# The attention section of a two-layer decoder trunk in another written-out order of its 1,026 steps

## The chip, the cores and the metric

The kernel runs on one core of one Trainium2 chip. The metric is the device time of one execution in microseconds. Shown are the median and the spread of three runs, and one profiled execution from which every row below is taken.

## What is computed

The reference is a decoder trunk with two layers for 256 tokens of width 1024, all in float32: a recurrent block, an MLP, sparse attention, an MLP, each behind an RMS norm and added to the residual, and a last norm.

```python
D_MODEL, SEQ, DEPTH, D_FF, N_HEADS, HEAD_DIM = 1024, 256, 2, 4096, 16, 64
def reference(...):
    for i in range(DEPTH):
        h = _rmsnorm(x, norm_mix[i])
        x = x + (_rglru_mixer(h, ...) if i % 2 == 0 else _nsa_mixer(h, ...))
        h = _rmsnorm(x, norm_ffn[i])
        x = x + jnp.square(jax.nn.relu(h @ mlp_w_up[i])) @ mlp_w_down[i]
    return _rmsnorm(x, norm_final)
# _nsa_mixer: q, six key/value projections and gates from h @ w_in; three branches
# (compressed keys, selected blocks, sliding window), each a masked softmax with
# ALiBi slopes, times its gate; their sum (16 heads x 64) @ w_out
```

## The kernel before

**Numbers in two parts.** Float32 products are made of parts: a value is its rounded part "hi" and the rest "lo", and x·w is hi·hi + hi·lo + lo·hi. Each weight piece (128x1024, 512 KB) is loaded into one of five buffers `raw0` to `raw4` by the queue of the SyncE engine (SP), rounded to `hi` by ScalarE (ACT) or VectorE (DVE) ("hi-split", L426), and its rest is made by VectorE ("lo-split", `whl<-raw,whl`, L423; L369 in the MLP). Piece i lies in `raw[i mod 5]`, and in one of seven hi/lo pairs in the tile `whl`. Four pieces (`BY_DMA`) are made otherwise: the GpSimd queue (POOL) loads hi with a cast, an engine multiplies it by -1 into lo (L491), and a second POOL transfer adds the weights to it (L493).

**The attention section** (L920 to the end of `trunk_kernel`'s second block) does the projections (`ks0 kw0 q0 ...`), the scores, softmax steps (L1297 is the rescaling of a block of probabilities), transposes with a copy `pth` (L1311), the products with the values (L1340, gathered into `osum` by L1344 on ACT and L1347 on DVE, then split into `oh` and `ol`), and the output projection in two halves `out0` and `out1` of eight column blocks m0 to m7. Each block of `out1` ends in a bank of the product memory and is added to the residual `xt` by DVE (L633, `xt<-xt,bank`). Blocks m0 to m7 of `out1` use the banks 2, 3, 4, 0, 1, 2, 3, 4.

**The lead-in.** The section's last part holds the first four pieces of the second MLP's up-projection, up1.0 to up1.3 (weight pieces 117 to 120, banks 0 to 3, 24 products of 128x256 each, L413 to L415), the norm for it (`hhl`, `acc`, L552 to L568), and, under `ahead`, the splits of the next three pieces 121 to 123 (`raw1`, `raw2`, `raw3`), which only the MLP behind the section reads. Piece 117 is in `raw2`, 118 in `raw3`, 119 in `raw4`, 120 in `raw0`; the last half of `out1`'s weights (`o13`, for m6 and m7) is piece 116, one of the four made by POOL.

**What sets the order.** A section collects its steps with `add(...)`; a step has one or two engines that may run it, and a function that issues its instructions. `emit` then calls the steps one by one. Each engine runs its instructions in the order in which they were issued, and each queue of transfers as well; waits between engines follow from the data. For the attention section the order is the text `ORDER`: step numbers, where `'` takes a step's second engine.

```python
sec.add("dve", 1.14, diff(lo, raw, hi), ...)      # a lo-split, one step
sec.emit(ORDER)                                    # the section's last line
```

Of the kernel before, what the change touches and what calls it, by code (L numbers as in the profile page):

```python
# [37 lines left out]
W1T, THS, THD, TPV, THT, NEARLY = 8.0, 10.5, 6.4, 44.0, 5.6, 6  # L38
SEED = (45, 94848, 51544, 88889, 49550, 67068, 32457, 33019)
ORDER = """  # L40
2 4 10 11 19 7 20 1 21 6 82 22 30 88 12 75 13 31 14 15 181 32 89 16 33 17 23 90 92 34 41 38' 35 24' 27 40 42 98 83 43 44
99 194 50 223 164 45 51 242 28' 36 46' 52 26 25 47 39 53 29 18 37 69 54 71 165 64 57 59 183 70 62 73 321 65 55 76 60 67
72 56 78 68 184 74 61 77 63 123 196 48' 79 376 58 80 126 124 81 66 49 118 84 225 121 85 197 86 127 94 122 87 119 426 108
125 96 109 91 226 114 93 128 153 120 148 110 129 95 154 480 244 133 97 9 130 151 135 0 101 131 3 134 103 323 100 149 102
136 142 137 105 111 152 207 115 141 104 156 106 139 324 140 107 166 157 378 167 138' 143 245 168 155 161 147 379 158 505
112 169 162 566 185 116 170 159 612 113 186 172 163 187 428 160 146' 212 144' 174 145' 188 213 173' 150 220 198 221 208
189 482 217 175 429 199 190 200 117 171 678 201 191' 193 227 202 222 192 228 204' 218 229 205 215 230 176 219 206 180'
# [6 lines left out]
422 342 486 360 473 435' 361 343 444 509 362 345 447 344 415 718 363 346 445 487 364 418 471 455 719 365 488 366 419  # L54
347' 456 367 416 489 457 368 402 348 474 490 417 369 570 494 492 458 405 401' 571 478 406 449 436 459 460 407 450 475
479 495 510 408 461 453 438 572 409 462 476 440 452 537 451 464 463 497 573 538 465 467 442 466 539 534 904 511 468 574
535 784 499 512 575' 454 500 536 502 524 529 513 501 503 761 585 588 514 540 887 515 530 541 519 586 525 542 531 520 527
616 532 545 587 517 528 617 888 543 522 631 533 618 965 589 546 619 576 526 544 632 590 973 504 591 560 633 596 981 547
927 549 594 561 580 592 658 583 548 563 550 595 599 578 682 593 551 597 581 600 634 552 620 564 648 553 562 565' 701 635
554 649 598 555 685 651 636 556 652 691 621' 686 606 557 688 624 607 650 659 626 608 558 687 629 610 660 559 692 689 627  # L60
601 694 663 602 622 690 661 603 611 928 710 738 609 604 711 713 605 695 989 712 906 653 1003 664 637 662 714 656 665 654
724 657 638 666 696 655 639 715 683 786 667 640 702 668 699 672 641 787 669' 725 642 671 684 945 700 643 726 697 721 644
# [3 lines left out]
823 818 796 837 833 821 835 807 794' 824 795' 822 819 789 825 817 842 802 803 808 797' 834 826 804 843 845 827 840 790  # L66
805 844 846 830 831' 847 848 828 841 838 863 806 836 849 829' 839 947' 850 864 866 857 791 896 948 867 858 865 859 909
861' 862 860' 853 868 869 851 917 854 870 852 872 871 889 873 875 874 809 876 855' 967' 877 856 929 880 878 897 881 983
890 879 918 882' 930 975 883 910 968 931 891 898 892 919 1007 899 911 937 900 912 1005 976 938 939 950 893 1006 895 1011
951 884 958 894 952 901 959 960 932 1009 1015 984 915 1010 991 1018 933 940 977 902 953 913 992 985 941 1016 920 1020  # L70
961 903 1022 914 923 1024 916 921 934 962 922 993 954 924 935 969 942 943 963 994 936 955 978 956 944 970 957 964 979
1013' 980 997 1014 971 998 986 999 1000 972 995 1001 996 1002 987 1017 988
"""
ROUNDS, SHIFT, MOVES, SPREAD = 6, 1.5, 12, 3.0
HPEN, LPEN, APEN, LEAD = 0.56, 1.0, 0.0, 9.0
# [1491 lines left out]
```

## Time and profile before

| what | value |
|---|---|
| median of three runs | 563.41 us (563.34 to 563.67) |
| the profiled execution's own time | 563.77 us |
| its span in the trace | 562.0 us (1.77 us lie around it) |
| attention section on TensorE (PE), by the timeline | 254.84 to 395.17 us |
| busy share of the span: PE / DVE / ACT / POOL | 98% / 81% / 69% / 9% |
| mean granted clock of TensorE | 0.993 |

Times in rows are microseconds from the start of the span unless they say ns. A row of a timeline is: start, duration, engine, source line, operation, output<-inputs, shape, count of instructions in the row, and in brackets the idle time of the engine just before it and what ended it. TensorE's products are pipelined: a product's duration is longer than its distance to the next one.

### The profile page before, as it was taken

Reading aid. Unit: us, or ns where it says so; the run is one execution under the profiler, and the core shown is the slowest. Engines: PE = TensorE matmul, PEld = TensorE weight load, DVE = VectorE, ACT = ScalarE, POOL = GpSimd, SP = SyncE. Lnnn points to the kernel's source line nnn. Section 1 sums busy time; section 2 is a strip of 40 time slices with the busy share of each in tenths; the row PEclk is TensorE's granted clock in tenths of the full one; section 3 lists DMA queues with packets and bytes.
Section 4 is the critical chain, followed back from the end, with each engine's and each line's share of the span. In section 5 each row is a group of like instructions: output and inputs, shape, how many; then the busy total and the mean of one; then the engine's idle time right before and its main releaser. Section 6 shows DMA issues by size and latency. Waiting matters only on the chain.

```text
span 562.0 us, 10531 instructions
## 1 busy us (share of the span) xinstructions
PE 549.1 (98%) x3862; PEld 517.2 (92%) x3862; DVE 455.8 (81%) x946; ACT 387.4 (69%) x790; POOL 51.1 (9%) x63
## 2 busy tenths in 40 slices
PE   9999999999999999999999998998999999999994
PEld 8999999999999999999999997998999999999994
DVE  6999999999995665767999999998899996565532
ACT  7699776877775543545999999974887776453420
POOL 1210000000000211311000101000000000142220
PEclk9999999999999999999999999998999999999998
DMA  8936366665555566556642585445576566456402
GB/s 300 398 125 197 147 224 204 247 219 188 206 207 188 180 207 212 186 187 229 237 152 66 154 234 168 96 94 195 166 234 213 197 213 217 160 193 212 157 1 75
DMA packets 32611, 105.19 MB, mean 187 GB/s; under 512 B 3984, under 2 KB 6944, under 8 KB 32560
## 3 DMA queue, kind: packets, MB, share of 16 engines
q1 hardware_dynamic: 30784, 99.70, 52.4%
q0 software_dynamic: 1200, 4.29, 3.4%
q8 instruction: 30, 0.49, 0.3%
q10 hardware_dynamic: 576, 0.53, 0.3%
q14 instruction: 21, 0.17, 0.1%
HBM read 101.36 MB, written 1.05 MB: 182 GB/s over the span
## 4 chain that ended last, share of the span: by engine, by line
PE 93%; DVE 2%; ACT 2%; DMA 1%; issue 1%; SPq 0%; DVEq 0%
PE bank L419 35%; PE bank L420 18%; PE bank L415 9%; PE bank L413 9%; PE bank L414 9%; PE bank L790 2%; PE bank L1308 2%; PE bank L1335 1%; PE bank L1268 1%; PE bank L1269 1%; DMA raw<-in_dram 1%; DVE whl L423 1%; PE bank L1139 1%; PE bank L1140 1%; PE bank L1138 1%; ACT whl L426 1%
## 5 line engine op out<-in xcount | busy, mean ns | idle before, releaser
L369 DVE TENSOR_TENSOR whl<-raw,whl 128x1024 fp32r<-128x1024 f32 x117 | 146.5, 1272 | 5.9 <-ACT whl L360 3.1
L419 PE MATMUL bank<-hhl,whl 128*128 128x512 f32 x456 | 149.4, 382 | 0.0
L419 PE MATMUL bank<-uhl,whl 128*128 128x512 f32 x448 | 146.8, 382 | 0.0
L360 ACT CAST whl<-raw 128x1024 fp32r<-128x1024 f32 (+1 forms) x118 | 120.5, 1046 | 7.8 <-ACT whl L360 5.7
L420 PE MATMUL bank<-hhl,whl 128*128 128x256 f32 x456 | 124.3, 273 | 0.0
L420 PE MATMUL bank<-uhl,whl 128*128 128x256 f32 x448 | 122.1, 273 | 0.0
L419 PEld LDWEIGHTS bank<-hhl,whl 128*128 128x128 f32 x456 | 86.2, 189 | 11.9
L419 PEld LDWEIGHTS bank<-uhl,whl 128*128 128x128 f32 x448 | 84.7, 189 | 11.8
L413 PE MATMUL bank<-hhl,whl 128*128 128x256 f32 x312 | 88.9, 285 | 1.7 <-DVE xt L633 1.7
L420 PEld LDWEIGHTS bank<-hhl,whl 128*128 128x128 f32 x456 | 87.6, 192 | 0.0
L415 PE MATMUL bank<-hhl,whl 128*128 128x256 f32 x312 | 86.9, 279 | 0.4 <-DVE whl L423 0.2
L414 PE MATMUL bank<-hhl,whl 128*128 128x256 f32 x312 | 86.8, 278 | 0.0
L420 PEld LDWEIGHTS bank<-uhl,whl 128*128 128x128 f32 x448 | 86.0, 192 | 0.0
L633 DVE TENSOR_TENSOR xt<-xt,bank 128x256 f32<-128x256 f32 x40 | 16.1, 414 | 72.3 <-ACT part L921 58.8
L423 DVE TENSOR_TENSOR whl<-raw,whl 128x1024 fp32r<-128x1024 f32 (+3 forms) x69 | 72.4, 1071 | 0.7 <-ACT whl L426 0.4
L413 PEld LDWEIGHTS bank<-hhl,whl 128*128 128x128 f32 x312 | 60.4, 194 | 2.2 <-issue 1.9
L426 ACT CAST whl<-raw 128x1024 fp32r<-128x1024 f32 (+2 forms) x62 | 58.0, 957 | 6.4 <-DMA raw<-in_dram 3.8
L415 PEld LDWEIGHTS bank<-hhl,whl 128*128 128x128 f32 x312 | 60.5, 194 | 1.0 <-DVE whl L423 1.0
L414 PEld LDWEIGHTS bank<-hhl,whl 128*128 128x128 f32 x312 | 60.4, 194 | 0.6 <-DVE hhl L683 0.2
L921 ACT COPY part<-bank 128x256 f32<-128x256 f32 x14 | 5.2, 373 | 61.8 <-PE bank L420 61.8
L886 ACT COPY b<-bank 128x256 f32<-128x256 f32 x57 | 21.0, 368 | 21.4 <-PE bank L420 21.3
L893 ACT ACTIVATE u<-t 128x256 f32<-128x256 f32 x64 | 26.7, 418 | 10.6 <-DVE t L891 5.0
(222 smaller groups left out, 998.3 us busy)
## 6 DMA issues: line engine op xcount, KB each, us to landing
raw<-in_dram SPq DMA_DIRECT2D x171, 512.0 KB, 4.1
whl<-in_dram POOLq DMA_DIRECT2D x8, 512.0 KB, 5.6
gw<-in_dram SPq DMA_DIRECT2D x4, 512.0 KB, 8.3
raw<-in_dram SPq DMA_DIRECT2D x5, 256.0 KB, 5.1
xt<-in_dram SPq DMA_DIRECT2D x4, 256.0 KB, 4.3
zwol<-in_dram SPq DMA_DIRECT2D x2, 512.0 KB, 5.8
raw<-in_dram SPq DMA_DIRECT2D x2, 456.0 KB, 4.0
kh<-th SPq DMA_DIRECT2D x8, 64.0 KB, 2.2
```

Of the source, the lines that this page charges most:

```text
L360: (act.copy if eng is None else eng.tensor_copy)(hi_t[i % NSPL][:, :n], raw_t[i % NRAW][:, :n])
L369: (eng or dve).tensor_tensor(lo[:, :n], raw_t[i % NRAW][:, :n], hi[:, :n].bitcast(F32), op=OP.subtract)
L413: pe.matmul(ps, wh, xh, start=start, stop=False)
L414: pe.matmul(ps, wh, xl, start=False, stop=False)
L415: pe.matmul(ps, wl, xh, start=False, stop=stop)
L419: pe.matmul(z.rearrange("p (i b a) -> p i b a", i=2, a=2), wh, xd, start=start, stop=False)
L420: pe.matmul(pairs(z[:, :S]), wl, xd[:, 0], start=False, stop=stop)
L423: return lambda e: e.tensor_tensor(o, a, h.bitcast(F32), op=OP.subtract)
L426: return lambda e: (e.copy if e is act else e.tensor_copy)(o, a)
L633: dve.tensor_tensor(two(xt[:, m]), two(xt[:, m]), nat(z), op=OP.add)
L886: act.copy(two(b), nat(z[:, S:]))
L893: act.activation(u, t, AF.Square)
```

## The change

Only the text `ORDER` differs. It holds 958 numbers, those of the 1,026 steps that issue something on an engine or a queue (the other 68 stand for the transfers that they start); the same 958 stand in another order, 41 of them with the other choice of engine. Products, shapes and buffers are the same; the lines of numbers tell nothing by themselves, so the first two are shown, and then what three places of the resulting programs look like.

```diff
@@ -38,38 +38,38 @@
 ORDER = """
-2 4 10 11 19 7 20 1 21 6 82 22 30 88 12 75 13 31 14 15 181 32 89 16 33 17 23 90 92 34 41 38' 35 24' 27 40 42 98 83 43 44
+1 4 11 19 7 10 20 2 21 3 22 30 88 12 75 13 31 14 82 15 181 89 32 16 33 17 23 90 98 91 24' 83 92 41 27 18 42 34 194 29 43
...
```

**VectorE at the end of the section, before.** These are its instructions from the split of piece 118 on (`raw3`); `raw4` is piece 119 (up1.2), `raw0` piece 120 (up1.3), `raw1` and the `raw2` here are the pieces 121 and 122 that only the MLP reads. `bank1_..` to `bank4_..` are the blocks of `out1`, `hhl` is the norm's lo part.

```order
L423 TENSOR_TENSOR whl_84<-raw3_81,whl_84 128x1024
L423 TENSOR_TENSOR whl_84<-raw1_79,whl_84 128x1024
L553 SCALAR_TENSOR_TENSOR hhl_93<-xt_88,vec_87,hhl_93 128x256 x2
L633 TENSOR_TENSOR xt_88<-xt_88,bank1_4560 128x256
L423 TENSOR_TENSOR whl_84<-raw4_82,whl_84 128x1024
L423 TENSOR_TENSOR whl_84<-raw2_80,whl_84 128x1024
L633 TENSOR_TENSOR xt_88<-xt_88,bank2_4609 128x256
L633 TENSOR_TENSOR xt_88<-xt_88,bank3_4626 128x256
L423 TENSOR_TENSOR whl_84<-raw0_78,whl_84 128x1024
L633 TENSOR_TENSOR xt_88<-xt_88,bank0_4521 128x256
L633 TENSOR_TENSOR xt_88<-xt_88,bank4_4641 128x256
```

**The same place of VectorE with the change**, from the split of piece 119 to that of piece 120.

```order
L423 TENSOR_TENSOR whl_84<-raw4_82,whl_84 128x1024
L553 SCALAR_TENSOR_TENSOR hhl_93<-xt_88,vec_87,hhl_93 128x256 x2
L633 TENSOR_TENSOR xt_88<-xt_88,bank2_4611 128x256
L633 TENSOR_TENSOR xt_88<-xt_88,bank0_4494 128x256
L423 TENSOR_TENSOR whl_84<-raw3_81,whl_84 128x1024
L553 SCALAR_TENSOR_TENSOR hhl_93<-xt_88,vec_87,hhl_93 128x256 x3
L633 TENSOR_TENSOR xt_88<-xt_88,bank3_4638 128x256
L563 TENSOR_TENSOR acc_94<-acc_94,sq1_99 128x256
L553 SCALAR_TENSOR_TENSOR hhl_93<-xt_88,vec_87,hhl_93 128x256
L423 TENSOR_TENSOR whl_84<-raw0_78,whl_84 128x1024
```

Further on, these are VectorE's last five rows of the section with the change; the next one is the MLP's first.

```order
L568 TENSOR_TENSOR acc_94<-acc_94,sq1_99 128x256
L423 TENSOR_TENSOR whl_84<-raw1_79,whl_84 128x1024
L544 RECIPROCAL rcol_96<-rcol_96 128x2
L423 TENSOR_TENSOR whl_84<-raw2_80,whl_84 128x1024
L423 TENSOR_TENSOR whl_84<-raw3_81,whl_84 128x1024
```

The splits of the pieces 121, 122 and 123 now stand behind the norm's last sum, the residuals of the banks 2 and 0 stand before the split of piece 118, and that of piece 119 stands ahead of it.

**ScalarE at the end of the attention, before**: the last two copies of transposes, the copies of the last value product, and the hi-splits of the pieces 119 and 118.

```order
L1311 CAST pth_2885<-bank5_4516 128x384
L1311 CAST pth_2885<-bank6_4531 128x384
L1344 COPY osum_2882<-bank7_4544 64x256 x2
L426 CAST whl_84<-raw4_82 128x1024
L426 CAST whl_84<-raw3_81 128x1024
```

**The same with the change.**

```order
L1311 CAST pth_2885<-bank5_4515 128x384
L1311 CAST pth_2885<-bank6_4520 128x384
L491 ACTIVATE whl_84<-whl_84 128x1024
L426 CAST whl_84<-raw3_81 128x1024
L1344 COPY osum_2882<-bank7_4545 64x256 x2
```

The multiplication by -1 of piece 116 (L491), which stood on VectorE, is now here, between the transposes' copies and the copies of the last value product; so is the hi-split of piece 118.

**The queue of SyncE while the last queries are moved, before**: `sa`, `sb` are the halves of the queries' tiles, filled by moves from `th` and `tl`; the others are loads of weight pieces.

```order
L346 DMA raw2_80<-in_4_dram 128x1024
L465 DMA sa2_2860<-th1_2875 64x256
L346 DMA raw3_81<-in_4_dram 128x1024
L346 DMA raw4_82<-in_4_dram 128x1024
L465 DMA sb2_2864<-tl1_2877 64x256
L465 DMA sb2_2864<-th1_2875 64x256
L465 DMA sa2_2860<-tl1_2877 64x256
L465 DMA sb3_2865<-th0_2874 64x256
```

**The same with the change.**

```order
L346 DMA raw2_80<-in_4_dram 128x1024
L465 DMA sa2_2860<-tl1_2877 64x256
L465 DMA sb2_2864<-tl1_2877 64x256
L465 DMA sa2_2860<-th1_2875 64x256
L465 DMA sa3_2861<-th0_2874 64x256
L465 DMA sb3_2865<-th0_2874 64x256
L465 DMA sb2_2864<-th1_2875 64x256
L465 DMA sb3_2865<-tl0_2876 64x256
L465 DMA sa3_2861<-tl0_2876 64x256
L346 DMA raw3_81<-in_4_dram 128x1024
L346 DMA raw4_82<-in_4_dram 128x1024
```

The loads of the pieces 118 and 119 (`raw3`, `raw4`) moved from between the moves of the last two queries to behind all of them.

## Rows read from the trace of the kernel before

**Rows 1.** The page's first section: busy time, share of the span and number of instructions of each engine.

```profile
PE 549.1 (98%) x3862; PEld 517.2 (92%) x3862; DVE 455.8 (81%) x946; ACT 387.4 (69%) x790; POOL 51.1 (9%) x63
```

**Rows 2.** Busy time in five stretches of the section. The columns are the stretch and its length, then the busy time (and number of instructions) of PE, the weight loads PEld, DVE, ACT and POOL, the granted clock of TensorE, the busy share of the transfer engines, and GB/s.

```profile
267.00:300.00 33.00, 33.00 (x280) 32.66 (x279) 32.38 (x86) 31.64 (x74) 0.87 (x6) 1.00 0.47 165
300.00:330.00 30.00, 29.57 (x244) 28.55 (x243) 28.85 (x119) 27.88 (x86) 2.79 (x5) 1.00 0.57 156
330.00:346.00 16.00, 14.52 (x105) 12.77 (x104) 15.73 (x66) 15.85 (x51) 0.00 (x0) 1.00 0.68 206
346.00:371.20 25.20, 25.20 (x201) 23.94 (x201) 24.42 (x106) 22.80 (x77) 3.21 (x4) 1.00 0.48 102
379.70:390.50 10.80, 8.86 (x61) 8.51 (x62) 10.70 (x23) 6.02 (x14) 0.00 (x0) 0.84 0.59 207
```

**Rows 3.** TensorE's timeline from its first product of the lead-in (up1.0) to a product of the MLP's fourth piece; `hhl,whl` is a product of up1, L419 one of the MLP behind the section.

```profile
379.65 0.35 PE L413 MATMUL bank<-hhl,whl 128*128 128x256 f32 x1
...
380.28 0.28 PE L415 MATMUL bank<-hhl,whl 128*128 128x256 f32 x1
382.25 0.35 PE L413 MATMUL bank<-hhl,whl 128*128 128x256 f32 x1 [1.70 <-DVE xt L633]
...
383.10 0.28 PE L414 MATMUL bank<-hhl,whl 128*128 128x256 f32 x1
383.62 0.58 PE L415 MATMUL bank<-hhl,whl 128*128 128x256 f32 x1 [0.25 <-DVE whl L423]
...
387.14 0.27 PE L413 MATMUL bank<-hhl,whl 128*128 128x256 f32 x1
...
390.38 0.28 PE L415 MATMUL bank<-hhl,whl 128*128 128x256 f32 x1
...
395.17 0.38 PE L419 MATMUL bank<-hhl,whl 128*128 128x512 f32 x1
...
403.03 0.38 PE L419 MATMUL bank<-hhl,whl 128*128 128x512 f32 x1
```

**Rows 4.** TensorE alone in four stretches of that time: stretch, length, its busy time (number of products), granted clock, busy share of the transfer engines, GB/s.

```profile
379.60:382.20 2.60, 0.95 (x7) 1.00 0.33 104
382.20:383.60 1.40, 1.13 (x8) 1.00 0.76 296
383.60:387.10 3.50, 3.48 (x16) 0.51 0.73 229
387.10:390.45 3.35, 3.35 (x32) 1.00 0.58 234
```

**Rows 5.** VectorE's timeline at the end of the section and into the MLP.

```profile
372.13 0.85 DVE L1347 TENSOR_TENSOR osum<-osum,bank 64x256 f32<-64x256 f32 x2 [0.61 <-ACT osum L1344]
...
373.68 1.22 DVE L423 TENSOR_TENSOR whl<-raw,whl 128x1024 fp32r<-128x1024 f32 x1
374.82 1.29 DVE L633 TENSOR_TENSOR xt<-xt,bank 128x256 f32<-128x256 f32 x3
...
378.30 0.88 DVE L553 SCALAR_TENSOR_TENSOR hhl<-xt,vec,hhl 128x256 fp32r<-128x256 f32 x2
379.09 0.41 DVE L633 TENSOR_TENSOR xt<-xt,bank 128x256 f32<-128x256 f32 x1
379.42 2.35 DVE L423 TENSOR_TENSOR whl<-raw,whl 128x1024 fp32r<-128x1024 f32 x2
381.69 0.74 DVE L633 TENSOR_TENSOR xt<-xt,bank 128x256 f32<-128x256 f32 x2
...
393.77 0.76 DVE L882 SCALAR_TENSOR_TENSOR t<-bank,rstd 128x256 f32<-128x256 f32 x2 [2.28 <-ACT rstd L546]
...
397.59 2.36 DVE L369 TENSOR_TENSOR whl<-raw,whl 128x1024 fp32r<-128x1024 f32 x2 [0.51 <-ACT whl L360]
```

**Rows 6.** The making of piece 116 and what stands around it: VectorE's multiplication, ScalarE's last copies, POOL's issue of the adding transfer, the times from issue to landing of POOL's eight weight transfers, and the groups of ScalarE's three multiplications of that kind elsewhere and of its hi-splits (busy, mean ns of one, idle before).

```profile
365.25 0.68 DVE L491 TENSOR_SCALAR whl<-whl 128x1024 fp32r<-128x1024 f32 x1
366.80 0.87 POOL L493 DMA_DIRECT2D whl<-in_dram  x1 [16.58 <-PE bank L1308]
DMA to landing us min/median/max: 3.9/5.6/9.2
368.96 0.48 ACT L1311 CAST pth<-bank 128x384 fp32r<-128x384 f32 x1 [0.22 <-PE bank L1308]
371.35 0.74 ACT L1344 COPY osum<-bank 64x256 f32<-64x256 f32 x2 [1.91 <-PE bank L1340]
L491 ACT ACTIVATE whl<-whl 128x1024 fp32r<-128x1024 f32 x3 | 3.2, 1051 | 0.0
L426 ACT CAST whl<-raw 128x1024 fp32r<-128x1024 f32 (+2 forms) x62 | 58.0, 957 | 6.4 <-DMA raw<-in_dram 3.8
```

**Rows 7.** The middle of the section: the group of VectorE's rescales (busy, mean ns of one, idle before), the two longest waits of TensorE there, the issue of two weight loads on SP's queue (pieces 118 and 119), and the times from issue to landing of the moves into `sa` between 300 and 400 us.

```profile
L1297 DVE TENSOR_SCALAR pt<-pt,sm 128x128 f32<-128x128 f32 (+1 forms) x19 | 5.5, 310 | 0.0
341.48 0.41 PE L1246 MATMUL bank<-cst,cq 128*64 128x128 f32 x2 [0.69 <-DVE cq L1228]
342.87 0.46 PE L1268 MATMUL bank<-kh,sa 128*128 128x512 f32 x1 [0.66 <-PE bank L1308]
333.56 1.02 SPq L346 DMA_DIRECT2D raw<-in_dram  x2
DMA to landing us min/median/max: 1.9/2.9/6.1
```

More of the change, by code (lines that the diff above doesn't have):

```diff
@@ L40 @@
 ORDER = """
-2 4 10 11 19 7 20 1 21 6 82 22 30 88 12 75 13 31 14 15 181 32 89 16 33 17 23 90 92 34 41 38' 35 24' 27 40 42 98 83 43 44
-99 194 50 223 164 45 51 242 28' 36 46' 52 26 25 47 39 53 29 18 37 69 54 71 165 64 57 59 183 70 62 73 321 65 55 76 60 67
-72 56 78 68 184 74 61 77 63 123 196 48' 79 376 58 80 126 124 81 66 49 118 84 225 121 85 197 86 127 94 122 87 119 426 108
-125 96 109 91 226 114 93 128 153 120 148 110 129 95 154 480 244 133 97 9 130 151 135 0 101 131 3 134 103 323 100 149 102
@@ L45 @@
-136 142 137 105 111 152 207 115 141 104 156 106 139 324 140 107 166 157 378 167 138' 143 245 168 155 161 147 379 158 505
-112 169 162 566 185 116 170 159 612 113 186 172 163 187 428 160 146' 212 144' 174 145' 188 213 173' 150 220 198 221 208
-189 482 217 175 429 199 190 200 117 171 678 201 191' 193 227 202 222 192 228 204' 218 229 205 215 230 176 219 206 180'
[6 rows of a table removed]
-422 342 486 360 473 435' 361 343 444 509 362 345 447 344 415 718 363 346 445 487 364 418 471 455 719 365 488 366 419
-347' 456 367 416 489 457 368 402 348 474 490 417 369 570 494 492 458 405 401' 571 478 406 449 436 459 460 407 450 475
@@ L56 @@
[L56 to L60, printed above, removed]
@@ L61 @@
-601 694 663 602 622 690 661 603 611 928 710 738 609 604 711 713 605 695 989 712 906 653 1003 664 637 662 714 656 665 654
-724 657 638 666 696 655 639 715 683 786 667 640 702 668 699 672 641 787 669' 725 642 671 684 945 700 643 726 697 721 644
[3 rows of a table removed]
-823 818 796 837 833 821 835 807 794' 824 795' 822 819 789 825 817 842 802 803 808 797' 834 826 804 843 845 827 840 790
-805 844 846 830 831' 847 848 828 841 838 863 806 836 849 829' 839 947' 850 864 866 857 791 896 948 867 858 865 859 909
-861' 862 860' 853 868 869 851 917 854 870 852 872 871 889 873 875 874 809 876 855' 967' 877 856 929 880 878 897 881 983
@@ L69 @@
[L69 to L72, printed above, removed]
+1 4 11 19 7 10 20 2 21 3 22 30 88 12 75 13 31 14 82 15 181 89 32 16 33 17 23 90 98 91 24' 83 92 41 27 18 42 34 194 29 43
@@ new lines @@
+38' 223 99 28 44 25 50 45 242 26 51 46 36' 164 35' 69 47 37 52 165 53 64 54 321 59 67 93 55 62 95 48 60 70 56 183 65 72
+71 39 184 74 57 77 66 118 61 79 119 376 123 121 120 49 73 126 76 40 196 81 124 78 58 68 80 197 153 225 148 84 151 426 86
+156 127 149 85 226 110 87 157 207 94 114 108 97 122 480 109 244' 101 128 152 96 129 100 150 111 132 102 6 323 130 133
+208 134 103 210 135 9 131 105 0 166 125 154 63 107 115 155 104 136 142 106 137 211 140' 167 139' 378 245 168 141 169 143
+116 175 505 324 138 185 428 161 170 158 566 112 146' 186 145' 162 144' 113 187 159 429 174 188 173 198 189 172 176 163
@@ new lines @@
+199 193 379 200 482 201 160 612 190 227 117 678 178' 192 202 217 228 483 507 229 171 191' 230 205 204' 246 231 203 247
+147' 234' 235 248 508 206 249 218 232 212 233' 325 568 250 213 220 255 215 251 219 209 569 253 256 614 257 252 221 615
+216 258 179 177 222 268 259 326 261 269 214 260 273 262 180 263 254 327 270 236 264 276 328 265 271 277 266 237 380 267
+329 680 285' 278 330' 283' 370 333 274 279 373 282 281 284 381 280 335 331 272 681 240 286 336 275 338 241 299 310 290
+238 758 287 291 382 311 300 288 292 313 430 301 312 289 315 296 383 314 302 293 297 349 716 303 354 384 294 304 239 340
@@ new lines @@
+350 385 305 357 341 306 390 355 371 352 392 431 307 374 394 885 356 308 410 375 432 351 397 309 411 358 316 484 413 395
+317 353 298 423 386 414 399 318 295 433 388 319 400 372 424 469 925 402' 718 320 485 434 425 342 401 719 359 435 472 343
+440 444 412 420 360 509 445 403 361 345 344 438 486 421 362 346 404 436 415 363 422 760 487 447 364 418 455 365 347 488
+366 419 416 456 367 489 348 474 417 368 492 494 457 477 475 369 470 570 490 458 405 449 478 406 495 571 450 476 460 442
+451 479 407 452 534 497 461 408 572 535 459 471 409 573 454' 462 537 536 473 904 464 510 574 538 784 463 453 524 467 575
@@ new lines @@
+511 465 527 468 525 512 466 539 528 580 540 526 499 513 887 761 588 585 529 586 616 500 514 532 501 530 541 515 503 519
+531 587 542 520 617 589 888 522 543 631 533 618 517 544 632 965 619 590 545 502 633 581 596 504 620 591 927 583 560 634
+546 576 592 549 561 621 594 599 564 622 597 563 550 593 626 648 658 562 551 629 651 595 552 685 649 635 578 553 565' 547
[6 rows of a table added]
+840 823 800 792 839 831' 807 793 822 824 789 794 796' 803 825 801 842 797' 832 795 828' 808 804 843 829' 830 845 844 790
+731 802 846 835 863 841 833 848 847 805 732 834 866 791 836 849 806 864 857 850 858 865 867 917 862 861' 859' 909 860
@@ L73 @@
+868 853 809 869 851 872 854 870 889 852 873 871 896 947 874 875 967' 975 948 876 855' 856 877 983' 910 880 890 878 881
+918 879 929 882' 930 883 897 968 919 891 931 892 911 1007 932 898 893 912 937 895 899 991 984 938 939 900 958 933 901
[3 rows of a table added]
 """
```

18 rows, old and new, of the table ORDER are left out of this document.

## The prediction

> **What bounds the kernel now.** I began with the page's first section: TensorE is busy for 98% of the span, so its own work is the floor and only its waits can be won; the other engines have room on average [rows 1]. An average over stages with different limits says little here, so the table of stretches came next. In the attention section it shows three engines full at once: from 267 to 300 VectorE has 32.38 of 33.00 us and ScalarE 31.64; from 330 to 346 they have 15.73 and 15.85 of 16.00, and there TensorE is idle for 16.00 - 14.52 = 1.48 us [rows 2]. In the middle a step can thus only be moved from one full engine to another. At the end it is otherwise: from 379.7 to 390.5 TensorE has 8.86 of 10.80 us at a mean granted clock of 0.84, VectorE is full (10.70), and ScalarE has only 6.02 [rows 2].
>
> The timeline of TensorE says what happens there [rows 3]. The products of the lead-in follow each other at 0.112 us (387.14 to 390.38 is 29 steps in 3.24). Six are done by 380.28; the next starts at 382.25, held by `xt` of L633, which is the residual that must read bank 2 before up1.2 may write it. That is 1.97 - 0.11 = **1.86 us**. VectorE's timeline shows why the residual is late: two lo-splits of 1.135 us each stand right ahead of it, from 379.42 [rows 5]. By the order they are those of piece 119, which up1.2 needs, and of piece 122, which only the MLP reads. The next stop is at 383.62, held by a lo-split of `whl`: 383.62 - 383.10 - 0.11 = **0.41 us** [rows 3]. After these stops the granted clock falls: 0.51 from 383.60 to 387.10, which is 1.2 of 2.4 GHz, and 1.00 before and behind [rows 4]. Sixteen products take 387.14 - 383.62 = 3.52 us instead of 16 x 0.112 = 1.79: **1.73 us** [rows 3, 4]. Together the tail loses 4.00 us. As a check: 379.65 to 395.17 is 15.52 us, the 96 products of the four pieces need 10.75, and the rest, 4.77, leaves 0.77 for the norm's few small products [rows 3].
>
> **The change part by part.**
>
> *The tail.* With the change the splits of 121 to 123 stand behind the norm, and the residuals of the banks 2 and 0 stand ahead of the split of 118. I walk VectorE from the split of piece 117, which starts at 373.68 before [rows 5], with its own steps from start to start: a lo-split 1.135 (two from 379.42 to 381.69), a residual 0.335 (379.09 to 379.42), a norm part 0.395 (two from 378.30 to 379.09). Lo-split 117, four residuals, lo-split 119, two norm parts and two residuals are 1.135 + 1.34 + 1.135 + 0.79 + 0.67 = 5.07, so 378.75, and TensorE wants the first product of up1 at 379.65: 0.9 early, some 0.7 after the step from engine to engine (a product starts about 0.15 behind what releases it; 382.25 stands so behind the end of the residual that starts at 381.69). Next, the split of 118 ends at 379.9, and up1.1 follows 12 products behind 379.65, at 381.0: 1.0 early. Three more norm parts, a residual, a sum, a norm part and the split of 120 end at 383.3; up1.3 comes 48 products behind, at 385.0. Each step is early by 0.7 to 1.7, so both stops go, and with them the fall of the clock: -1.86 - 0.41 - 1.73 = **-4.00**. The rows bear out that short waits leave the clock alone: it was 1.00 over the waits of 0.69 and 0.66 near 342 [rows 2, 7].
>
> If VectorE comes to the tail a full 1.0 us late, the first stop returns with about 0.3 to 1.0 us, and perhaps the clock's fall with it.
>
> *What the splits do where they are now.* Three lo-splits, 3.4 us, end VectorE's row in front of the MLP. Before, the MLP's first instruction there, at 393.77, had waited 2.28 for ScalarE's `rstd` [rows 5], so this gap covers most of it; VectorE comes some 2 us later relative to TensorE. The split of piece 124 ran from 397.59, 2.4 behind TensorE's first MLP product (395.17), and is read at 403.03, 7.9 behind it [rows 3, 5]. Two later is 4.4 to 5.6 for its end: 2.3 us left. I cost it at nothing; without that cover it is 2 x 1.135 = 2.27.
>
> *The middle.* The numbers of instructions by engine differ a little. Ahead of the last `ol` split VectorE gets four more rescales (0.31 each, [rows 7]) and two more hi-splits, and gives up the multiplication L491, which has the size of a hi-split (0.68, [rows 6]), and, net, some seven copies of 128x256, which I price like a rescale, the nearest row. That is 4 x 0.31 + 0.68 - 7 x 0.31 = **-0.25**. VectorE is the fuller engine from 346 to 371 (24.42 of 25.20, [rows 2]), so I take the whole. Below, the order could win all of TensorE's idle time from 300 to 346, 0.43 + 1.48 = 1.9 [rows 2]; above, the two longest waits there, 0.69 + 0.66, could come a second time, 1.35 [rows 7].
>
> *Piece 116.* Its multiplication goes from VectorE to ScalarE, behind the last copies of transposes (368.96 + 0.48) and takes 1.05 there; the hi-split of 118 follows (0.95, about the mean of its kind), so ScalarE is free for `osum` at 371.44, which started at 371.35 after an idle 1.91 [rows 6]: **+0.1**. POOL issued the adding transfer 0.87 behind the multiplication (366.80 against 365.93) [rows 6]; now at 370.49 + 0.87 = 371.4. With the median landing of 5.6 it is there at 377.0. Its first reader, the products of m6 and m7, 24 x 0.112 = 2.7 ahead of 379.65, comes at 377.0 [rows 3, 6]. So this transfer, which had 4.6 us to spare (366.80 + 5.6 = 372.4), has none. At the median I cost it at nothing; at the shortest landing (3.9) it is 1.7 early, at the longest (9.2) 3.6 late.
>
> A rule bears on this. The Trainium skill's page "SBUF — State Buffer", section "SBUF: two separate sides", says that while VectorE runs a float32 copy from SBUF to SBUF, GpSimd cannot write the descriptors of a transfer that it issues. The new place is next to VectorE's hi-split of 119, so by the rule the transfer could start up to one such copy later, 0.7 us by the trace, and be that late; the trace of before has one issue of 0.87 us, and no run here shows the lock. By the rule alone the sum would be 0.7 higher.
>
> *SP's queue.* The loads of 118 and 119 leave the moves of the last two queries ahead of them. The moves into `sa` took 1.9 to 6.1 us with the two loads issued in front at 333.56; the score product at 342.87 had waited 0.66 [rows 7]. This could give back up to 0.66, but VectorE and ScalarE are full there, and I take 0. The loads are wanted near 370, some 28 us behind their new place: no loss.
>
> **The sum.** -4.00 - 0.25 + 0.1 = -4.15. The profiled execution took 563.77, so 559.62; that execution lies 0.36 above the median of 563.41, so the median is forecast at 559.26, **559.3**.
>
> **The rivals.**
>
> *The stop shrinks but stays.* VectorE arrives a microsecond late at the lead-in, by new waits in the middle. For it: it is full all the way, so each wait of its own goes through; against it: its work ahead is no longer than before. With 1.0 us of wait the time is 560.3, with the clock's fall too 562.0.
>
> *The splits are paid back in the MLP*, because VectorE doesn't catch up there: +2.27, 561.5. Against it: 81% busy over the span [rows 1], and 2.3 us in hand.
>
> *The middle wins too*, most of its 1.9: 557.6.
>
> *A new wait in the middle* of the size of the tail's, with a fall of the clock: 1.86 + 1.73, so 562.9; no change.
>
> *Piece 116 lands late* (the other side). Its transfer takes the longest landing of the rows, 9.2: the products of m6 wait 3.6 us, and the clock falls (1.73): 559.3 + 5.3 = 564.6, slower. It decides from a landing of about 9.2 on; with a clock that holds it is 562.9. For it: no time in hand; against it: the median is 5.6, and the stretch before it moves 102 GB/s, the least of the five [rows 2, 6].
>
> *The change does nothing*: VectorE's queue is the same work, and the stop only goes to another product: 563.3. Against it: 3.4 us of splits leave the path for a gap of 2.28 and the MLP's slack.
>
> **How the numbers follow.** A difference under 0.2%, 1.1 us, is what a measurement of this kernel can't tell from none. The forecast has 0.58 (own range 558.2 to 560.4: the small terms of the middle and 0.7 by piece 116); the middle wins too 0.10; the stop shrinks but stays 0.14; paid back in the MLP 0.06; a new wait in the middle 0.05; does nothing 0.03; piece 116 late 0.04. Under 562.3 lie the first four, 0.88; within 0.2% the next two, 0.08; above, 0.04. The range 557.3 to 562.0 leaves out the last three, 0.12, and the edges of the others.
>
> **What would show it.** In the changed trace the first products of up1 should run without a stop over 0.3 us, at a granted clock of 1.00, and the MLP's first product should come near 391.0 instead of 395.17. The residual of bank 2 should end before TensorE's first up1 product. The first instruction of the MLP on VectorE should show a smaller wait than 2.28, and TensorE no wait for `whl` of L369 in the next 10 us. `whl` of POOL should hold up no product of m6. The stretch 330 to 346 should keep about its 1.5 us of idle. I am wrong if a stop of over 1 us stands before the lead-in or in it, or if the MLP starts by 391 but the end doesn't come earlier by as much.

## The result and the profile after

The changed kernel takes **560.29 us** (median of 4 runs, 559.74 to 560.97) against 563.54 for the kernel before in the same comparison: a ratio of 0.9941, 95% interval 0.9924 to 0.9958, or 3.25 us less. The forecast was 559.3, in a range of 557.3 to 562.0. The profiled execution took 560.43 us (span 558.6), 3.34 less than the one before. One thing is needed to read the medians below: kernels with before's order on SP's queue take 2 to 6 us more in some of their executions, which is taken up at the runs `tail_sp` and `A_sp`.

The page's first row of after, to set beside [rows 1]:

```profile
PE 547.1 (98%) x3862; PEld 515.5 (92%) x3862; DVE 454.8 (81%) x943; ACT 387.3 (69%) x793; POOL 51.0 (9%) x63
```

The five stretches of [rows 2] in the changed kernel, with the same columns:

```profile
267.00:300.00 33.00, 32.84 (x278) 32.23 (x277) 32.12 (x87) 30.07 (x69) 1.00 (x7) 1.00 0.47 163
300.00:330.00 30.00, 29.83 (x245) 28.57 (x245) 28.83 (x120) 28.11 (x93) 2.58 (x4) 1.00 0.59 158
330.00:346.00 16.00, 14.65 (x108) 13.13 (x107) 15.67 (x61) 15.83 (x47) 0.00 (x0) 1.00 0.63 192
346.00:371.20 25.20, 24.70 (x196) 23.39 (x195) 24.35 (x104) 24.79 (x82) 2.45 (x4) 1.00 0.37 90
379.70:390.50 10.80, 10.80 (x99) 10.80 (x99) 10.24 (x22) 8.19 (x15) 0.00 (x0) 1.00 0.43 146
```

The last row is the change: 10.80 of 10.80 us busy at a granted clock of 1.00, where before it was 8.86 at 0.84. But TensorE now also stands where it did not: 0.16 us from 267 to 300 and 0.50 from 346 to 371.2, both 0.00 before. From 300 to 346 it stands a little less, 1.52 us against 1.91.

TensorE's timeline, the section's first product, the first of up1 and the first of the MLP, for [rows 3]:

```profile
255.15 0.28 PE L413 MATMUL bank<-hhl,whl 128*128 128x256 f32 x1
...
380.43 0.28 PE L413 MATMUL bank<-hhl,whl 128*128 128x256 f32 x1
...
391.73 0.46 PE L419 MATMUL bank<-hhl,whl 128*128 128x512 f32 x1
```

And TensorE alone between them, for [rows 4]:

```profile
380.40:391.70 11.30, 11.30 (x103) 1.00 0.49 156
```

These two starts split the result. The lead-in takes 391.73 - 380.43 = 11.30 us instead of 15.52, a gain of 4.22. But it begins at 380.43 instead of 379.65, 0.78 later. Of this, 0.31 was there when the section began, at 255.15 instead of 254.84. TensorE's first product of the first layer, far ahead of the section, already starts at 6.23 us instead of 5.94, so this part comes from the two executions and not from the order. The part of the section ahead of the lead-in lost the other **0.47**. Together that is -3.44, and the rest of the program hardly moves. I call the part ahead the head, and the part from the split of piece 117 on the tail.

VectorE's timeline at the end, for [rows 5]:

```profile
379.19 0.74 DVE L633 TENSOR_TENSOR xt<-xt,bank 128x256 f32<-128x256 f32 x2
379.85 1.22 DVE L423 TENSOR_TENSOR whl<-raw,whl 128x1024 fp32r<-128x1024 f32 x1
...
383.24 1.22 DVE L423 TENSOR_TENSOR whl<-raw,whl 128x1024 fp32r<-128x1024 f32 x1
...
390.06 2.34 DVE L423 TENSOR_TENSOR whl<-raw,whl 128x1024 fp32r<-128x1024 f32 x2
392.42 0.76 DVE L882 SCALAR_TENSOR_TENSOR t<-bank,rstd 128x256 f32<-128x256 f32 x2
...
396.18 1.23 DVE L369 TENSOR_TENSOR whl<-raw,whl 128x1024 fp32r<-128x1024 f32 x1 [0.51 <-ACT whl L360]
```

The two residuals end before TensorE's first product at 380.43, the splits of 118 and 120 come in time, and the wait of 2.28 us in front of the MLP's first instruction (L882) is gone, filled by the splits at 390.06. The split of piece 124 starts 4.45 us behind the MLP's first product (2.42 before), as the walk had it.

The four waits of TensorE in the middle of the changed kernel, for the two in [rows 7]:

```profile
337.25 0.35 PE L1268 MATMUL bank<-kh,sb 128*128 128x256 f32 x1 [0.40 <-PE bank L1205]
341.64 0.45 PE L1268 MATMUL bank<-kh,sa 128*128 128x512 f32 x1 [0.58 <-PE bank L1340]
345.39 0.48 PE L1268 MATMUL bank<-kh,sb 128*128 128x512 f32 x1 [0.30 <-DVE pc L1249]
347.29 0.45 PE L1268 MATMUL bank<-kh,sb 128*128 128x512 f32 x1 [0.50 <-DVE mx L1275]
```

All four are score products (L1268). Before, two waits of 0.69 and 0.66 stood there, 1.35 in all; now it is 1.78 in four. Two of the four are put down to TensorE's own earlier products (L1205, L1340), so what ended them is not shown.

ScalarE's part of piece 116 and POOL's issue, for [rows 6]:

```profile
369.71 1.06 ACT L491 ACTIVATE whl<-whl 128x1024 fp32r<-128x1024 f32 x1
...
372.27 0.74 ACT L1344 COPY osum<-bank 64x256 f32<-64x256 f32 x2 [0.56 <-PE bank L1340]
```

```profile
371.06 0.85 POOL L493 DMA_DIRECT2D whl<-in_dram  x1 [21.03 <-ACT whl L491]
```

### The profile page after: what moved, and what is told of

Same layout as the page of the kernel before. It is cut to its first block, busy times and chain, and to the rows that moved or that the text cites. A ratio compares the mean times of both kernels' runs of the same rounds, so it can differ in the third digit from the quotient of the medians.

```text
span 558.6 us, 10523 instructions
## 1 busy us (share of the span) xinstructions
PE 547.1 (98%) x3862; PEld 515.5 (92%) x3862; DVE 454.8 (81%) x943; ACT 387.3 (69%) x793; POOL 51.0 (9%) x63
## 4 chain that ended last, share of the span: by engine, by line
PE 90%; ACT 5%; DVE 2%; DMA 1%; issue 1%; SPq 0%; DVEq 0%; ACTq 0%
PE bank L419 35%; PE bank L420 18%; PE bank L414 9%; PE bank L413 9%; PE bank L415 9%; PE bank L790 2%; ACT pt L1278 2%; PE bank L1308 1%; DMA xt<-in_dram 1%; ACT pth L1311 1%; PE bank L1335 1%; PE bank L1268 1%; PE bank L1140 1%; PE bank L1138 1%; PE bank L1139 1%
## 5 line engine op out<-in xcount | busy, mean ns | idle before, releaser
L419 PE MATMUL bank<-hhl,whl 128*128 128x512 f32 x456 | 149.5, 382 | 0.0
L419 PE MATMUL bank<-uhl,whl 128*128 128x512 f32 x448 | 146.8, 382 | 0.0
L419 PEld LDWEIGHTS bank<-hhl,whl 128*128 128x128 f32 x456 | 86.2, 189 | 11.9
L419 PEld LDWEIGHTS bank<-uhl,whl 128*128 128x128 f32 x448 | 84.7, 189 | 11.8
L893 ACT ACTIVATE u<-t 128x256 f32<-128x256 f32 x64 | 26.7, 418 | 12.3 <-DVE t L891 7.1
```

The lines of the kernel that those rows point to most:

```text
L419: pe.matmul(z.rearrange("p (i b a) -> p i b a", i=2, a=2), wh, xd, start=start, stop=False)
L893: act.activation(u, t, AF.Square)
```

## The experiments

The first four runs ask where the 3.3 us come from. A run's edit is told as what it does to `ORDER`, where `B` is before's list of numbers and `A` the changed one.

### tail_of_after and head_of_after

```diff
-ORDER = B
+ORDER = B[:863] + [x for x in A if x not in B[:863]]     # tail_of_after
+ORDER = A[:863] + [x for x in B if x not in A[:863]]     # head_of_after
```

The entry at 863 is the lo-split of piece 117, in both lists.

> The order of before up to the last `ol` split of the attention, and from the split of piece 117 on the order of the changed kernel. If head and tail add up (theory A: the tail gives 4.0 to 4.2 us, the changed order ahead of it loses 0.8), this is 563.5 - 4.1 = 559.4 us, 0.8 under the changed kernel, with no stop over 0.3 us in the lead-in and a granted clock of 1.00. Rival (B: the stop went only because TensorE came 0.8 us later to the lead-in in the changed kernel): a stop of 0.3 to 1.0 us at the lead-in, 560.0 to 561.5.

> The changed kernel's order up to the last `ol` split, and before's order from the split of piece 117 on. Theory A: the new head costs 0.8 us and the tail loses its 4.0 again, 564.3 us. Rival (the head costs nothing and the tail gave only 3.3): 563.5.

Measured: tail_of_after **559.7 us** (ratio 0.9934, 0.9913 to 0.9956), head_of_after **564.47** (1.0009, 0.9996 to 1.0022; the kernel before had 563.9 in this comparison). By the traces the lead-in of tail_of_after takes 11.31 us and begins at 379.55, as early as before; the MLP begins at 390.86, 0.87 ahead of the changed kernel. Its section begins at 254.88, 0.27 ahead of the changed kernel's, so 0.60 of the 0.87 belong to the new head; the medians, 559.7 and 560.29, say the same, and so do 564.47 and 563.9. So head and tail add up, theory A: the tail gives 4.2, the new head costs 0.5 to 0.6, less than the 0.8 that theory A had. The rival (B) falls, since the stop goes without a later TensorE.

head_of_after shows something more. It has before's tail with the same two stops, but its clock did not fall. TensorE in the stretch where before's clock was 0.51:

```profile
384.60:388.10 3.50, 3.20 (x23) 1.00 0.76 238
```

And its waits in the lead-in:

```profile
383.15 0.35 PE L413 MATMUL bank<-hhl,whl 128*128 128x256 f32 x1 [1.69 <-DVE xt L633]
384.53 0.38 PE L415 MATMUL bank<-hhl,whl 128*128 128x256 f32 x1 [0.25 <-DVE whl L423]
387.05 0.38 PE L414 MATMUL bank<-hhl,whl 128*128 128x256 f32 x1 [0.30 <-DVE hhl L553]
391.05 0.61 PE L625 MATMUL bank<-ones,acc 128*128 128x1 f32 x4 [0.16 <-DVE acc L568]
...
395.83 0.38 PE L419 MATMUL bank<-hhl,whl 128*128 128x512 f32 x1
```

At the full clock two more waits for VectorE appear (`hhl`, `acc`), and the lead-in, from 380.55, still takes 15.28 us. Up to the second stop the two lead-ins agree within 0.01 us, counted from their first products (2.60 and 3.97 before, 2.60 and 3.98 here); then one clock falls and the other does not. So the fall in the kernel before cost 0.24 us, not 1.73: slow products only hid that VectorE's norm parts come late too.

### one_split and two_splits

```diff
-... 984 915 1010 991 1018 ... 986 999 1000 972 ...
+... 984 915 991 1018 ... 986 999 1000 1010 972 ...        # one_split: 1010, the lo-split of 122
+... and 1006, the lo-split of 121, behind 1000 as well     # two_splits
```

> The kernel before with one step moved: the lo-split of piece 122 goes from its place in front of the residual of bank 2 to behind the norm's reciprocal. VectorE reaches the residual 1.135 us earlier, so the stop of 1.86 shrinks to 0.73, and that of 0.41 stays. If a stop of this length lets the granted clock fall as before, 563.5 - 1.1 = 562.4 us; if the clock holds, as over the waits of 0.69 and 0.66 near 342, 1.73 more is won: 560.7.

> The kernel before with two steps moved: the lo-splits of the pieces 121 and 122 go behind the norm's reciprocal, and everything else stays. If these two alone made the stop, the residual of bank 2 comes 2.27 us earlier, both stops and the clock's fall go, and the time is 563.5 - 4.0 = 559.5 us. If the changed order of the residuals and of the splits of 118 and 119 is needed too, a stop of 0.4 or more stays: 560.2 or more. If the two splits are paid for behind the section, 561.8.

Measured: 563.2 us (0.9995, 0.9969 to 1.0021) and 563.07 (0.9987, 0.9963 to 1.0011), neither clear of no change. In both, the moved splits stand behind the loads that refill their buffers (1022 and 1024), so they split the wrong pieces; what follows the section says nothing. The lead-in stands ahead of that, and can be read. In one_split it takes 14.42 us with the clock at 1.00, 1.1 less than before, the length of one split, and holds four waits, the first two of which were 1.70 and 0.25 before:

```profile
381.03 0.38 PE L413 MATMUL bank<-hhl,whl 128*128 128x256 f32 x1 [0.47 <-DVE xt L633]
382.78 0.38 PE L415 MATMUL bank<-hhl,whl 128*128 128x256 f32 x1 [0.59 <-DVE whl L423]
```

The other two, of 0.30 and 0.16, are those of head_of_after. Beside head_of_after, at the same clock, the first stop is 1.22 shorter and the second 0.34 longer; that leaves 0.88, and the lead-in is 0.86 shorter. The clock held here, and the 1.73 that the expectation gave to a held clock did not come. In two_splits the lead-in takes 14.56 us: the second deferred split won nothing. Neither expectation had that; in the next runs the loads are moved along with the splits.

### three_splits and three_splits_hi

```diff
-... 893 1006 895 ... 915 1010 991 ... 903 1022 914 923 1024 916 ... 997 1014 971 998 ... 999 1000 972 ...
+... 893 895 ... 915 991 ... 903 914 923 916 ... 997 971 1006 998 ... 999 1000 1010 1014 1022 1024 972 ...
 # three_splits_hi, besides:
-... 900 912 1005 976 ... 915 991 1018 ...
+... 900 912 991 1005 976 ... 915 1018 ...
```

> The kernel before; the lo-splits of the pieces 121, 122 and 123 go to the places that they have in the changed kernel (121 behind the norm's last sum, 122 and 123 behind the reciprocal), with the loads that refill the buffers of 121 and 122 behind them; all else stays. Theory Q (the tail is VectorE's queue: three splits of 1.135 us are 3.4 us): the MLP's first product at 395.17 - 3.4 = 391.8, 560.2 us. Theory of the forecast (two stops and a fall of the clock, removed by the two splits that stood ahead of the residual): 391.2, 559.5. Rival (ScalarE, which makes the hi-split of piece 120 only behind those of 121 and 122, holds the lead-in next): stops of 0.5 and 0.9 us stay, 392.6, 561.0.

> The same as three_splits, and on ScalarE the hi-split of piece 120 moved ahead of those of 121 and 122, as in the changed kernel. If ScalarE's order matters, this run is 0.5 to 1.4 us under three_splits, with no stop over 0.3 in the lead-in: first MLP product near 391.0, 559.5 us. If VectorE's queue alone sets the end, the two are equal.

Measured: 562.69 us (0.9988, 0.9973 to 1.0003) and 563.17 (0.9984, 0.9962 to 1.0006) beside 563.86: 1.2 and 0.7 us of the 4 by the medians, with intervals that include no change. The lead-ins take 14.56 and 14.15 us. The waits of TensorE in the lead-in of three_splits:

```profile
381.74 0.38 PE L413 MATMUL bank<-hhl,whl 128*128 128x256 f32 x1 [0.35 <-ACT whl L426]
383.00 0.38 PE L415 MATMUL bank<-hhl,whl 128*128 128x256 f32 x1 [0.77 <-DVE whl L423]
```

ScalarE and VectorE of the same run at that time:

```profile
380.65 1.03 ACT L426 CAST whl<-raw 128x1024 fp32r<-128x1024 f32 x1
```

```profile
381.72 1.23 DVE L423 TENSOR_TENSOR whl<-raw,whl 128x1024 fp32r<-128x1024 f32 x1 [0.99 <-ACT whl L426]
```

VectorE is early now and stands 0.99 us for ScalarE's hi-split of piece 120, which comes at 380.65, behind the hi-splits of 121 and 122. This is the third theory, ScalarE's order, in its kind of stop but not in its size: it had the MLP's first product at 392.6, and it came at 394.30. Moving that one hi-split ahead (three_splits_hi) won 0.4 us in the lead-in, not the 0.5 to 1.4 expected, and the median is not lower: the hi-split then stands ahead of a norm part of ScalarE (L552), for which VectorE waits 1.18 us instead of 0.24. The profiled execution of three_splits_hi is one of the long ones (565.60 us).

### ahead_all

As three_splits, and ScalarE's hi-splits of 121 and 122 (1005, 1009) behind its last norm step:

```diff
-... 912 1005 976 ... 932 1009 984 ... 964 979 1013' 980 ...
+... 912 976 ... 932 984 ... 964 979 1005 1009 1013' 980 ...
```

> As three_splits (the lo-splits of 121 to 123 behind the norm), and ScalarE's hi-splits of 121 and 122 moved behind its last norm step too: all the work that only the MLP reads is held to the end, and the order of the residuals, of the splits of 117 to 120 and of the table load stays as before. Theory W: this is the whole of the tail's gain; no stop over 0.3 us in the lead-in, its length near 11.3 us (first product of up1 to first product of the MLP) against 15.5 before, 559.6 us. Rival: the order of the residuals and of the hi-split of 120 on ScalarE is needed too; stops of 0.5 to 1 us stay and the lead-in takes 12.3 us or more, 560.5 or more.

Measured: **561.62 us** (0.9967, 0.9942 to 0.9992). The lead-in takes 13.15 us. So holding back all work that only the MLP reads, on both engines, is worth 15.52 - 13.15 = 2.37 of the 4.22 us, and the order of the steps that the lead-in itself needs is worth the other 1.85: theory W falls, and the rival stands by its length (12.3 or more), though the stops that are left are shorter than the 0.5 to 1 that it had. The waits that are left are for VectorE's norm parts:

```profile
384.19 0.38 PE L414 MATMUL bank<-hhl,whl 128*128 128x256 f32 x1 [0.29 <-DVE hhl L553]
388.19 0.61 PE L625 MATMUL bank<-ones,acc 128*128 128x1 f32 x4 [0.15 <-DVE acc L568]
```

Which of those steps it is (the residuals' order, the split of 119 ahead of that of 118, ScalarE's table load of 1.28 us, or TensorE's own order of the four pieces) was not tried one by one. The traces point to TensorE's own order. The norm's last sum on VectorE (L568) is read by TensorE's small product L625. The sum in the kernel before, in ahead_all and in the changed kernel, there with L625:

```profile
389.67 0.42 DVE L568 TENSOR_TENSOR acc<-acc,sq 128x256 f32<-128x256 f32 x1
```

```profile
387.72 0.41 DVE L568 TENSOR_TENSOR acc<-acc,sq 128x256 f32<-128x256 f32 x1
```

```profile
388.20 0.42 DVE L568 TENSOR_TENSOR acc<-acc,sq 128x256 f32<-128x256 f32 x1
389.14 0.50 PE L625 MATMUL bank<-ones,acc 128*128 128x1 f32 x4
```

| kernel | start of L568, from the first product of up1 | first product of the MLP, from the start of L568 | lead-in |
|---|---|---|---|
| before | 10.02 | 5.50 | 15.52 |
| head_of_after | 10.03 | 5.25 | 15.28 |
| one_split | 9.16 | 5.26 | 14.42 |
| three_splits | 9.30 | 5.26 | 14.56 |
| three_splits_hi | 8.89 | 5.26 | 14.15 |
| ahead_all | 7.89 | 5.26 | 13.15 |
| the changed kernel | 7.77 | 3.53 | 11.30 |

In every kernel with before's order of these products and a full clock, the MLP begins 5.25 or 5.26 us behind the start of that sum, and only the sum's own time differs. In ahead_all the sum is as early as in the changed kernel, within 0.12. What is left is what TensorE has behind L625: 36 of the 96 products in before's order, 18 in the changed one, and 18 x 0.112 = 2.0 us. Counted this way the gain of 4.22 is 2.25 by the earlier sum and 1.97 by what stands behind it. This is read from the traces; no run moved TensorE's order alone.

### early_of_after and late_of_after

```diff
+ORDER = hybrid of A[:264], B up to step 863, then A      # early_of_after
+ORDER = B[:264] + [x for x in A if x not in B[:264]]      # late_of_after
```

> The changed kernel's order for the first 264 steps (up to the first products of the hidden layer, about 300 us), then before's order to the last `ol` split, then the changed tail. Its sister with before's order in the first part too had its first MLP product at 390.86 and the changed kernel has it at 391.73: the changed order ahead of the tail costs 0.87. If the part up to 300 us (two waits for score products at 274.6 and 277.1) makes half of it, 391.3 and 560.1 us; if it is hidden by later waits, 390.9 and 559.7.

> Before's order for the first 264 steps and the changed kernel's behind them. If the loss of 0.87 us comes from the part from 300 to 371 (the score products at 337, 345 and 347 wait for ScalarE's and VectorE's softmax steps there), the first MLP product is at 391.7 and the time 560.3 to 560.5 us as in the changed kernel; if from the part up to 300, 390.9 and 559.7.

Measured: 561.76 us (0.9961, 0.9935 to 0.9988; half of its ten runs lie near 560.4) and **560.88** (0.9949, 0.9934 to 0.9963). late_of_after has its first MLP product at 391.81, near the changed kernel's 391.73. Counted from the section's first product, it comes after 136.63 us there, 136.58 in the changed kernel and 135.98 in tail_of_after: the part behind 300 us suffices for the whole of the head's loss, with the score products' waits at 337, 345 and 347 again in its trace. early_of_after tells little: in its profiled execution a score product that reads `sa` waited 1.43 us near 344, which is more than any loss looked for.

### tail_sp and A_sp

```diff
 # tail_sp, from tail_of_after: the loads of 118 (973) and 119 (981) behind the moves of the queries
-... 632 590 973 504 ... 633 596 981 547 ... 602 622 690 ...
+... 632 590 504 ... 633 596 547 ... 602 622 973 981 690 ...
 # A_sp, from the changed kernel: the same two loads back between the moves
-... 633 581 596 ... 928 659 973 556 ... 650 660 981 693 ...
+... 633 581 973 981 596 ... 928 659 556 ... 650 660 693 ...
```

> As tail_of_after (before's order to the last `ol` split, the changed tail), and on SP's queue the loads of the pieces 118 and 119 moved behind the moves of the last two queries, as in the changed kernel. In tail_of_after two of twelve runs took 563 to 565 us, the others 559.2 to 560.2, and in every kernel with before's order of this part some runs do so; where the profile caught one, the score product near 343.5 had waited 1.4 to 1.7 us for the moves and the granted clock fell after it. Theory S: the two loads ahead of the moves make this wait; then the median stays near 559.6 and no run is over 561.5. Rival: the order of the score products makes it; then one or two runs of twelve still take 563 or more.

> The changed kernel with the loads of the pieces 118 and 119 put back on SP's queue to where they stood before, behind the first move of the seventh query. Theory S: median 560.3 or up to 0.7 more, and some of twelve runs at 563 or more, which the changed kernel and the other two kernels with its order of this part did not show in 20 runs. Rival: 560.3 with all runs under 561.5.

Measured: tail_sp **559.47 us** (0.9914, 0.9890 to 0.9938), all six runs from 559.27 to 560.41. A_sp **565.38** (1.0014, 0.9996 to 1.0031), all twelve from 564.01 to 566.90. With the changed order of the scores theory S stands, and is larger than thought: the two loads in front of the moves cost 5 us by the medians, and the shortest of the twelve runs is 3 us over the longest of the changed kernel. With before's order tail_sp agrees with it, but six runs are few. The wait in A_sp:

```profile
344.43 0.76 PE L1268 MATMUL bank<-kh,sa 128*128 128x512 f32 x1 [3.42 <-DMA sa<-th]
```

and TensorE behind it (stretch, length, busy, clock, transfers):

```profile
342.00:345.00 3.00, 0.57 (x2) 0.89 0.46 123
345.00:350.00 5.00, 5.00 (x24) 0.50 0.61 206
```

The score product waits 3.42 us for a move into `sa`; then the clock is at half. The times from issue to landing of the moves into `sa`, in A_sp, the changed kernel and tail_sp:

```profile
DMA to landing us min/median/max: 1.9/2.8/7.6
```

```profile
DMA to landing us min/median/max: 1.9/2.0/3.9
```

```profile
DMA to landing us min/median/max: 2.0/2.5/4.1
```

With before's order of the scores a wait at the same place comes only in some executions; the trace does not name what it was for. In two_splits (566.42 us) the profile caught one, and the clock fell after it:

```profile
343.69 0.60 PE L1268 MATMUL bank<-kh,sa 128*128 128x512 f32 x1 [1.38 <-issue]
```

```profile
344.00:350.00 6.00, 6.00 (x22) 0.50 0.48 178
```

In early_of_after (560.75 us) it caught one as long, and the clock held:

```profile
344.48 0.45 PE L1268 MATMUL bank<-kh,sa 128*128 128x512 f32 x1 [1.43 <-issue]
```

```profile
344.00:350.00 6.00, 5.52 (x39) 1.00 0.54 179
```

The two runs beside them show the same pair: three_splits waited 1.17 us there and kept its clock (562.88 us), three_splits_hi 1.19 and its clock fell to 0.52 (565.60 us). So in these profiles the wait alone does not make an execution long; the fall of the clock behind it does. In the profiled execution of tail_sp no score product waits for `sa` there.

All kernels with before's order of this part, counted together, took 2 us or more above their own fastest in 40 of 183 runs; the four kernels with the loads behind the moves (the changed one, head_of_after, late_of_after, tail_sp) in none of 26. For tail_sp alone it is none of 6, which a share of 40 in 183 would give about one time in five.

tail_sp is 4.41 us under the kernel before in its comparison, where the changed kernel is 3.25 under it; the two were not measured side by side. It is before's order with the changed tail and the two loads moved.

### dup_cover

```diff
-... 1014 ...
+... 1014 1014 1014 1014 1014 ...
```

> As tail_of_after, with the lo-split of piece 123 made five times instead of once at the end of the section (the same values each time): 4 x 1.135 = 4.5 us more for VectorE in front of the MLP. The forecast put the room there at 2.3 us: then 2.2 us show, in waits of the MLP's products for `whl`, 559.7 + 2.2 = 561.9. If the MLP has room for all of it 559.7; if it has none 564.2.

Measured: 562.7 us (0.9988, 0.9962 to 1.0014), 3.0 over tail_of_after. VectorE's row of splits in front of the MLP, and the MLP's first instruction behind it:

```profile
389.46 7.39 DVE L423 TENSOR_TENSOR whl<-raw,whl 128x1024 fp32r<-128x1024 f32 x6
396.76 0.75 DVE L882 SCALAR_TENSOR_TENSOR t<-bank,rstd 128x256 f32<-128x256 f32 x2
```

and the waits of the MLP's products:

```profile
397.24 0.48 PE L419 MATMUL bank<-hhl,whl 128*128 128x512 f32 x1 [0.61 <-DVE t L882]
400.58 0.48 PE L419 MATMUL bank<-hhl,whl 128*128 128x512 f32 x1 [0.46 <-ACT whl L360]
401.85 0.38 PE L420 MATMUL bank<-hhl,whl 128*128 128x256 f32 x1 [0.78 <-DVE whl L369]
```

L882 starts 5.62 us behind the MLP's first product (396.76 - 391.14) where it is 0.68 in tail_of_after (391.54 - 390.86): 4.94 later, and not 4.54, since a repeated split took 1.26 us instead of 1.135. From the MLP's first product to the end of the span it is 2.64 us longer (169.53 against 166.89). So 2.3 of the 4.94 us were hidden, the room that was forecast; by the medians, 3.0 of them show and 1.9 were hidden. One of the waits is of another kind than expected: a bank that L882 reads late.

## Why the prediction was right, and where not

The median came out at 560.29, 1.0 us above the forecast and at the upper edge of its main case (558.2 to 560.4). A rival, the stop that shrinks but stays, had 560.3; the trace excludes it, since no stop is left.

**The tail: right in size, half right in cause.** -4.00 was forecast and -4.22 came, all in the lead-in, with no stop and a clock of 1.00. The walk along VectorE held: the residuals ended 0.5 us ahead of TensorE, where 0.9 was worked out, with TensorE itself 0.8 later. But the step "two lo-splits make the stop, the stop makes the clock fall, and the three add up" is not what the runs show. Deferring the splits on VectorE alone gave 1.0 us, with ScalarE's hi-splits 2.4, and only the whole new tail 4.2. And the 1.73 of the clock was no loss of its own: at a full clock, head_of_after's lead-in is only 0.24 shorter. What bounded the lead-in was the norm's last sum at the end of VectorE's row and what TensorE had still to do behind it. The walk ended at the split of piece 120, ahead of that sum, and did not look at TensorE's order, which by the traces is worth 1.97 of the 4.22. That the three terms gave the right total is partly luck: together they are all that the lead-in took beyond its products at full clock, and the changed kernel takes all of it away, by two things of which the forecast had one.

**The middle: wrong.** The step that failed is the one that took VectorE's count of work, -0.25, for time, with +0.1 for `osum`: -0.15 in all, where the head lost 0.47, and 0.60 beside tail_of_after. From 346 to 371 VectorE is as full as it was (24.35 against 24.42), and still TensorE stands 0.50 longer: at 347.29 a score product waits for VectorE's `mx` (L1275), a softmax step. late_of_after shows that the order behind 300 us makes the loss; that it is the place of the score products in TensorE's row is argued from the waits at 337 to 347 and was not tried alone. With full engines the count of work did not tell the time. The upper bound of this term, +1.35, did hold it. `osum` was not delayed: ScalarE was free 0.56 us early, since TensorE came later.

**SP's queue: right for the profiled execution, and the most instructive miss.** I took 0 out of 0 to -0.66, since the engines were full there. The medians show little more: moving the two loads alone took tail_of_after from 559.7 to 559.47. But none of the 26 runs with the loads behind the moves is one of the executions that are 2 to 6 us longer, and for the changed order of the scores the move was needed: without it, +5.1 us (A_sp). The rows had the sign of it, landings of up to 6.1 us for moves behind two loads [rows 7]; I read the one wait of 0.66 and not the spread.

**Piece 116: not late.** POOL issued 0.29 us behind the multiplication instead of 0.87, and the transfer, at the median landing of 5.6, was there at 376.7 (it landed 5.5 us after its issue); its first reader came at 377.7. The rival on the other side did not come. The rule that I set beside it, the Trainium skill's page "SBUF — State Buffer", section "SBUF: two separate sides", is hardly put to the test: one of VectorE's hi-splits ran from 370.67 for 0.68 us, over the first 0.29 of POOL's issue from 371.06, and the next started at 371.92, behind it. The issue took 0.85, no longer than before's 0.87, so no lock shows here.

**The splits behind the section: right.** No product of the MLP waited for them; dup_cover puts the room near the 2.3 us of the forecast.

## What to carry to other kernels

A stop that the trace names can be only the first place where a late engine shows: before adding up waits, follow that engine's row to the end of the stretch and see what waits next at full clock, who waits for the engine that feeds it, and how much work the waiting engine still has behind the last thing that it waits for. Here that last count, 36 products or 18, was by the traces worth about as much (1.97 us) as the late engine's earlier end (2.25). When a stretch has several full engines, the count of work doesn't tell the time; a new order lost there even with less work. And on a queue of transfers read the longest landing, not the one wait that a profile caught: big loads ahead of small moves that a product waits for cost little in most executions of the kernel before and up to 5 us in others.

## What the runs showed of the hardware

The granted clock went to 0.50 (1.2 of 2.4 GHz) after a stand of 3.42 us (A_sp) and after one of 1.38 us with another of 0.68 close before it (two_splits). But early_of_after had stands of 0.68 and 1.43 us at the same place and kept a clock of 1.00, and the same stop, of 1.70 and 1.69 us, was followed by a fall in the kernel before and by none in head_of_after. Moves of 64 KB that stood behind two loads of 512 KB on one queue landed after up to 7.6 us (A_sp), and after up to 3.9 us (the changed kernel) and 4.1 us (tail_sp) without the loads ahead of them.
